# Four small edits at the start of a two-layer hybrid mixer: warm-up matmuls, an activation in front, two small writes elsewhere, modulation units in pairs

## The chip, the cores and the metric

The kernel runs on one core of a Trainium2 chip, as one program. The metric is the device time of one execution in microseconds (us). The median of three runs of the kernel before is 1768.27 us (1764.97 to 1769.26). One more execution was recorded by the profiler.

The engines are TensorE (PE; its weight loads are shown as PEld), VectorE (DVE), ScalarE (ACT), GpSimd (POOL) and SyncE (SP, which only issues DMAs here). DMAs issued by SyncE and by ScalarE appear as SPq and ACTq.

## The reference, cut to what matters

Two layers of a conditioned transformer-like block over 256 context and 256 latent tokens of width 1024. Each layer mixes three branches (a gated delta rule, a gated linear recurrence, a differential attention) and ends in a gated feed-forward. What bears on the change is the conditioning: a vector `c` (and one for the context, `c_ctx`) goes through a SiLU and a matrix of 6 times 1024 columns per layer; the six pieces shift, scale and gate the two sublayers.

```
s_lat = jax.nn.silu(c)
s_ctx = jax.nn.silu(c_ctx)[None]
for l in range(DEPTH):
    mod_l = jnp.split(s_lat @ w_mod[l] + b_mod[l], 6, axis=-1)
    mod_c = jnp.split(s_ctx @ w_mod[l] + b_mod[l], 6, axis=-1)
    u_l = modulate(rmsnorm(h_lat, norm_mix[l]), mod_l[0], mod_l[1])
    u_c = modulate(rmsnorm(h_ctx, norm_mix[l]), mod_c[0], mod_c[1])
    ...
```

Here `modulate(h, shift, scale)` is `h * (1 + scale) + shift`.

## The kernel before, in words

**Layout.** Activations lie feature-major: 8 tiles of 128 features by 512 tokens (256 of the context, then 256 latent). Every product of float32 accuracy is made of three matmuls in a rounded format: high part by high part, high by low, low by high (`gemm`, lines 271 to 273). A weight slab is loaded by SyncE (line 256), its high part is rounded (259) and its low part is the difference (260).

**First stage of layer 0 (lines 446 to 490).** The residual `h` is read in eight loads of 256 KB; ScalarE squares each and VectorE adds the squares up (`Norm.add`). Then come small constants, the conditioning vector (`s_in`, 128 KB), the parameter vectors. `s_act`, the SiLU of the conditioning vector, is made of a tanh on ScalarE (line 460) and two VectorE operations; it needs another table of ScalarE than the square root of the norm. Two DMAs on ScalarE's queue (line 464) write the two columns of `s_act`, 1,024 values of 4 bytes each, to a DRAM tile `sd`. It is read back, broadcast over the partitions, by `mod_steps` (line 328), where VectorE makes the other modulation pieces as row sums: first around 450 us of the span.

The shift and scale of the first sublayer are made by TensorE. Their 2048 columns are eight units of 256. A unit (`mod_unit`) loads 1 MB of weights (`wm`, six buffers), makes 8 matmuls in four column groups of the array (line 306), copies the bank to SBUF (`mev`, one buffer, line 308), makes two transposes (311) and a reduction over the groups (312), and adds the bias. The stage goes by quarters: quarter i takes units i and 4+i, loads the matching quarter of the weights of the first five projections (`w32`, 640 KB, line 475), modulates two of the eight tiles, and then adds that quarter's products to five PSUM banks (`pre`: two of `mm`, two of `pg`, one of `md`). After four quarters the five banks hold five finished projections, and layer 0 goes on with slabs.

**Layer 0 behind that.** The remaining projections of the delta rule, its chunks, then four projections of the recurrence and the rotated q and k of the attention (line 1011 on, `rope`), then the recurrent scans (`lru`), attention, the merge and the feed-forward.

**What sets the order.** The order on each engine is not the order of the text. A scheduler plays the program through with a model of the engines' and transfers' times: an instruction becomes ready when what it needs is done and its tile has a place, and an engine that is free takes the ready instruction that comes first in the text. `high_priority(offset=n)` moves instructions n places ahead for this choice (slab loads 300, modulation matmuls 60); `keep_in_program_order` ties one behind the instruction before it in the text on its engine. On the chip each engine then runs its list strictly in order. DMAs signal their landing on eight counters in turn, and a DMA waits until the one eight places before it has landed.

Of the kernel before, what the change touches and what calls it, by code (L numbers as in the profile page):

```python
# [9 lines left out]
F32 = mybir.dt.float32  # L10
F32R = mybir.dt.float32r
F16 = mybir.dt.float16
AF = mybir.ActivationFunctionType
# [8 lines left out]
YO = (3, 0, 4, 5, 1, 6, 7, 2)  # L22
EARLY = 6
NFIRST = 5
MB = 6
MW = 256
D = 1024
# [146 lines left out]
def build(tc, I, out, dbg=None):  # L174
    nc = tc.nc
    V, S, G, PE, SP = nc.vector, nc.scalar, nc.gpsimd, nc.tensor, nc.sync
# [14 lines left out]
    def nm(s):  # L191
        uid[0] += 1
        return f"{s}_{uid[0]}"

    def tap(name, ap):
        if dbg is not None:
            dbg(name, ap)
# [10 lines left out]
    def bank(tag="dn", dt=F32):  # L208
        return banks["pool"].tile([128, 512], dt, tag=tag, name=nm(tag), bufs=banks["n"][tag])
# [7 lines left out]
    def scope(name, side=None):  # L217
        p = tc.tile_pool(name=nm(name), bufs=1, side=side, reuse_waits="tile")
        q = p.__enter__()
        return q, lambda: p.__exit__(None, None, None)  # L220
# [6 lines left out]
    s_act = cp.tile([128, 8, 32], F32, name="s_act")  # L227
# [8 lines left out]
    def vc(l, name, j=0, n=1):  # L236
        o = l * NVL + _V[name] + j
        return vec[:, o:o + n]
# [46 lines left out]
    def mod_out(l, k0, nb, nv):  # L285

        o = modT[l][:, k0:k0 + nb, 0:nv]
        V.tensor_tensor(o, in0=o, in1=vc(l, "bm", k0, nb).unsqueeze(2).to_broadcast([128, nb, nv]), op=ALU.add)
        c, k = k0 // 8, slice(k0 % 8, k0 % 8 + nb)
        i = c // 3  # L290
        if c % 3 == 1:
            V.scalar_tensor_tensor(amod[l][i][:, k, 0:nv], in0=o, scalar=1.0, op0=ALU.add, op1=ALU.mult,
                                   in1=vc(l, ("nm", "nf")[i], k.start, nb).unsqueeze(2).to_broadcast([128, nb, nv]))
        if c % 3 == 2:
            V.tensor_scalar(gmod[l][i][:, k, 0:nv], in0=o, scalar1=0.5, scalar2=None, op0=ALU.mult)

    def mod_unit(q, tag, p, bufs):

        nb = MW // 128
        wm = p.tile([128, 8, MW], F32, tag="wm", name=nm("wm"), bufs=bufs)  # L300
        SP.dma_start(wm, I["wmod"][:, q * MW:(q + 1) * MW].rearrange("(a p) c -> p a c", p=128))
        ps = bank(tag)[:, :MW]
        with tc.high_priority(offset=60):
            for k in range(8):
                j = 32 * (k % 4)
                PE.matmul(ps[j:j + 32], lhsT=s_act[:, k], rhs=wm[:, k], start=k < 4, stop=k >= 4, tile_position=(0, j))
        ev = p.tile([128, MW], F32, tag="mev", name=nm("mev"), bufs=1)
        S.copy(ev, ps)
        pt = bank(tag)[:, :MW].rearrange("p (b f) -> p b f", f=128)
        for b in range(nb):  # L310
            PE.transpose(pt[:, b], ev[:, b * 128:(b + 1) * 128], ident)
        V.tensor_reduce(modT[0][:, q * nb:(q + 1) * nb], in_=pt.rearrange("p b (g r) -> p b r g", r=32)[:, :, 0:2], op=ALU.add,
                        axis=AX.X)
        mod_out(0, q * nb, nb, 2)

    sd = dp.tile([2, D], F32, name="sd")
# [84 lines left out]
    def new_u():  # L401
        return [[up.tile([128, 512], F32R, tag=t, name=nm(t)) for t in ("uh", "ul")] for _ in range(8)]

    def modulate(u, h, rs, l, which, tk, p, tag="nt", bufs=4, ks=range(8)):

        for k in ks:
            t = p.tile([128, 512], F32, tag=tag, name=nm("nt"), bufs=bufs)
            hi, lo = u[k]
            for sl, i in ((CTX, 1), (LAT, 0)):
                if tk in (ALL, sl):  # L410
                    a = amod[l][which][:, k, i:i + 1]
                    b = modT[l][:, which * 24 + k, i:i + 1]
                    if k % 2 == 0:
                        V.scalar_tensor_tensor(t[:, sl], in0=h[k][:, sl], scalar=a, in1=rs[:, sl], op0=ALU.mult, op1=ALU.mult)
                        S.activation(hi[:, sl], t[:, sl], AF.Identity, bias=b)  # L415
                        V.scalar_tensor_tensor(lo[:, sl], in0=t[:, sl], scalar=b, in1=hi.bitcast(F32)[:, sl], op0=ALU.add,  # L416
                                               op1=ALU.subtract)
                    else:
                        G.tensor_tensor(t[:, sl], in0=h[k][:, sl], in1=rs[:, sl], op=ALU.mult)
                        V.tensor_scalar(t[:, sl], in0=t[:, sl], scalar1=a, scalar2=b, op0=ALU.mult, op1=ALU.add)  # L420
                        S.copy(hi[:, sl], t[:, sl])
                        G.tensor_tensor(lo[:, sl], in0=t[:, sl], in1=hi.bitcast(F32)[:, sl], op=ALU.subtract)
# [18 lines left out]
    def new_h():  # L441
        t = [hp.tile([128, 4, 512], F32, tag="h", name=nm("h")) for _ in range(2)]
        return [t[k // 4][:, k % 4] for k in range(8)]


    sp, done_sp = scope("st")
    s_in = sp.tile([128, 8, 32], F32, name="s_in")
    h = new_h()
    nn = Norm(sp)
    u = new_u()  # L450
    first = ("mm", "mm", "pg", "pg", "md", "dn")[:NFIRST]
    nfst = len(first)
    pre = {n: bank(b) for n, b in enumerate(first)}
    for k in range(8):
        SP.dma_start(h[k], I["hin"][:, k])
        nn.add(k, h[k], ALL)
    SP.dma_start(cst[:, 0:256], I["cst"][:, 0:256])
    SP.dma_start(s_in, I["cc"])
    SP.dma_start(vec, I["vec"])
    S.activation(s_act, s_in, AF.Tanh, scale=0.5)  # L460
    V.scalar_tensor_tensor(s_act, in0=s_act, scalar=1.0, in1=s_in, op0=ALU.add, op1=ALU.mult)
    V.tensor_scalar(s_act, in0=s_act, scalar1=0.5, scalar2=None, op0=ALU.mult)
    for v in range(2):
        S.dma_start(sd[v].rearrange("(k p) -> p k", p=128), s_act[:, :, v])
    V.tensor_copy(id16, ident)
    V.tensor_scalar(neg16, in0=ident, scalar1=-1.0, scalar2=None, op0=ALU.mult)
    for r in HALVES:
# [1 line left out]
    rs, _ = nn.close(ALL)  # L469

    def quarter(i):
        mod_unit(i, "dn", sp, MB)
        mod_unit(4 + i, "dn", sp, MB)
        w32 = sp.tile([128, nfst, 2, 128], F32, tag="w32", name=nm("w32"), bufs=2)
        SP.dma_start(w32, I["w"][0, 0:nfst].rearrange("n p (k c) -> p n k c", k=8)[:, :, 2 * i:2 * i + 2])
        modulate(u, h, rs, 0, 0, ALL, sp, bufs=8, ks=range(2 * i, 2 * i + 2))
        return w32
# [13 lines left out]
    for l in range(L):  # L491
        full = l == 0
# [19 lines left out]
        def proj(n, tk, tag=None):  # L512

            if n in pre:
                return pre.pop(n)
            if tag is None:
                tag = rot[0]
                rot.append(rot.pop(0))
            ps = bank(tag)
            w = tk.stop - tk.start  # L520
            gemm(ps[:, :w], slab(l, n), range(8), u, tk)
            return ps[:, :w]
# [42 lines left out]
        dn, done_dn = scope("dn")  # L565
# [10 lines left out]
        def conv(ps, w, bias, y):  # L576

            n = ps.shape[1] // 256
            xp = xq.tile([128, 2, 260], F32, tag="xp", name=nm("xp"), bufs=2)[:, :n]
            pv = ps.rearrange("p (s t) -> p s t", t=256)  # L580
            yv = y.rearrange("p (s t) -> p s t", t=256)
            G.memset(xp[:, :, 0:1], 0.0)
            G.memset(xp[:, :, 257:259], 0.0)
            S.copy(xp[:, :, 1:257], pv)
            if bias is None:
                S.activation(yv, pv, AF.Copy, scale=w[:, 1:2])  # L586
            else:
                S.activation(yv, pv, AF.Identity, scale=w[:, 1:2], bias=bias)
            for j in (0, 2, 3):
                V.scalar_tensor_tensor(yv, in0=xp[:, :, j:j + 256], scalar=w[:, j:j + 1], in1=yv, op0=ALU.mult, op1=ALU.add)  # L590
# [138 lines left out]
        for j in range(2):  # L729
            p = proj(W_LX + j, ALL)  # L730
# [280 lines left out]
        for j in range(2, 4):  # L1011
            conv(proj(W_LX + j, ALL), vc(l, "lcw", 4 * j, 4), vc(l, "lcb", j), lx[:, j])
            tap(f"lx{l}", lx[:, j])
        for at, t4, tk in ((W_DQ, dq, TK), (W_DK, dk, ALL)):
            for j in range(4):
                rope(proj(at + j, tk), t4[:, j])
                tap(f"dqk{l}", t4[:, j])
# [94 lines left out]
        scale = 64 ** -0.5  # L1112
# [109 lines left out]
        nn = Norm(cq, sq="zs", rs="macc", nsq=1, nrs=2)  # L1222
# [21 lines left out]
        u, pre = by_halves(last, h, nn, l, 1, tks, cq, ((W_FF, "mm"), (W_FF + 1, "dn")), "ya", 8)  # L1244
# [25 lines left out]
        nn = Norm(fp)  # L1270
# [24 lines left out]
        if l == 0:  # L1295
            u, pre = by_halves(last, h, nn, 1, 0, tks, fp, FIRST)
# [34 lines left out]
```

## Time and profile before

| What | Value |
|---|---|
| median of three runs | 1768.27 us |
| profiled execution | 1766.63 us |
| its span, first to last instruction | 1764.8 us |
| granted TensorE clock, mean | 0.979 |
| TensorE matmul busy | 1642.2 us (93%) |
| VectorE busy | 1184.1 us (67%) |
| ScalarE busy | 781.7 us (44%) |
| GpSimd busy | 196.4 us (11%) |
| read from memory | 230.92 MB |

Busy shares are means over the whole span; a change in one stage is read from the rows of that stage. In a row of a timeline stand the start, the time from the first to the last end, engine, line, operation, tiles (out from in), and the number of instructions; in brackets the idle time of the engine ahead of it and what ended it. In a chain of waits stand start, length and what the time was spent on.

### The profile page before, as it was taken

The numbers are of one execution on the slowest core, as the hardware profiler recorded it, in microseconds if no ns is written. First come the engines' busy times: TensorE is split into PE (matmuls) and PEld (weight loads), VectorE is DVE, ScalarE is ACT, GpSimd is POOL, SyncE is SP. The second block draws the span as 40 slices with busy tenths as digits, with TensorE's granted clock in tenths as the row PEclk, the third lists the DMA queues.
The fourth block names the chain that finished last, engine by engine and source line by source line (L and its number), as shares of the span: only waits on it lengthen the run. The fifth ranks groups of instructions, "written<-read, shape, count | busy, mean of one in ns | idle before, by whom it ended". The sixth has DMA issues, their size and how long they took to land.

```text
span 1764.8 us, 28759 instructions
## 1 busy us (share of the span) xinstructions
PE 1642.2 (93%) x11346; PEld 1365.6 (77%) x11346; DVE 1184.1 (67%) x2033; ACT 781.7 (44%) x1326; POOL 196.4 (11%) x266
## 2 busy tenths in 40 slices
PE   4898999899999998999999999989999999989997
PEld 2676787567777887777778888767787599989997
DVE  4578665586887746899883337776666775765554
ACT  4475653656422234322223224667545634444443
POOL 1211100000310004111111003011000002111100
PEclk8999999999999998999999999999999999989999
DMA  9433101221655434566872334332113145545554
GB/s 243 142 132 98 44 20 41 96 71 37 196 180 179 161 113 137 179 200 206 278 235 93 107 107 145 108 128 66 50 38 111 48 142 187 185 146 187 183 180 131
DMA packets 100343, 235.18 MB, mean 133 GB/s; under 512 B 11072, under 2 KB 36556, under 8 KB 99568
## 3 DMA queue, kind: packets, MB, share of 16 engines
q1 hardware_dynamic: 88928, 228.46, 40.3%
q10 hardware_dynamic: 11280, 4.89, 1.2%
q8 instruction: 89, 1.46, 0.3%
q14 instruction: 46, 0.38, 0.1%
HBM read 230.92 MB, written 2.39 MB: 132 GB/s over the span
## 4 chain that ended last, share of the span: by engine, by line
PE 47%; DVE 18%; issue 16%; DMA 10%; ACT 5%; POOL 2%; SPq 1%; POOLq 0%; DVEq 0%; ACTq 0%
PE mm L272 7%; PE mm L273 7%; PE mm L271 7%; DVE md L347 5%; PE dn L273 4%; PE dn L271 4%; PE dn L272 4%; DVE wl L260 4%; DMA mwm<-in_wmt 3%; PE dn L802 2%; PE dn L816 2%; DMA f<-in_wmt 2%; PE pp L1061 1%; DMA wm<-in_wmod 1%; PE dn L913 1%
## 5 line engine op out<-in xcount | busy, mean ns | idle before, releaser
L260 DVE TENSOR_TENSOR wl<-wr,wh 128x1024 fp32r<-128x1024 f32 (+1 forms) x299 | 368.3, 1232 | 228.4 <-PE dn L273 91.6
L259 ACT CAST wh<-wr 128x1024 fp32r<-128x1024 f32 (+1 forms) x241 | 249.2, 1034 | 360.1 <-PE dn L272 184.9
L273 PE MATMUL mm<-uh,wl 128*128 128x512 f32 (+1 forms) x1048 | 372.1, 355 | 17.2 <-DVE wl L260 17.0
L271 PE MATMUL mm<-uh,wh 128*128 128x512 f32 (+1 forms) x1048 | 372.6, 355 | 4.3 <-ACT uh L415 2.5
L272 PE MATMUL mm<-ul,wh 128*128 128x512 f32 (+1 forms) x1048 | 370.3, 353 | 2.5 <-DVE ul L416 2.1
L273 PEld LDWEIGHTS mm<-uh,wl 128*128 128x128 f32 x1048 | 201.2, 192 | 48.8 <-DVE wl L260 24.1
L271 PEld LDWEIGHTS mm<-uh,wh 128*128 128x128 f32 x1048 | 201.6, 192 | 32.4 <-issue 6.4
L272 PEld LDWEIGHTS mm<-ul,wh 128*128 128x128 f32 x1048 | 201.4, 192 | 32.4 <-issue 6.7
L273 PE MATMUL dn<-uh,wl 128*128 128x512 f32 (+1 forms) x448 | 153.2, 342 | 1.5 <-DVE wl L260 1.5
L271 PE MATMUL dn<-uh,wh 128*128 128x512 f32 (+1 forms) x448 | 152.7, 341 | 0.0
L272 PE MATMUL dn<-ul,wh 128*128 128x512 f32 (+1 forms) x448 | 152.6, 341 | 0.0
L347 DVE SCALAR_TENSOR_TENSOR md<-mwm,sb 128x512 f32<-128x512 f32 x160 | 124.4, 778 | 14.5 <-DMA mwm<-in_wmt 10.9
L273 PEld LDWEIGHTS dn<-uh,wl 128*128 128x128 f32 x448 | 86.0, 192 | 13.4 <-DVE wl L260 4.5
L272 PEld LDWEIGHTS dn<-ul,wh 128*128 128x128 f32 x448 | 86.1, 192 | 9.2
L271 PEld LDWEIGHTS dn<-uh,wh 128*128 128x128 f32 x448 | 86.2, 192 | 8.7
L347 DVE SCALAR_TENSOR_TENSOR md<-f 128x512 f32<-128x512 f32 x96 | 76.1, 792 | 19.2 <-DMA f<-in_wmt 14.0
L277 POOL TENSOR_TENSOR hid<-ft,hid 128x512 fp32r<-128x512 f32 (+1 forms) x44 | 50.9, 1158 | 332.9 <-ACT hid L276 332.9
L276 ACT CAST hid<-ft 128x512 fp32r<-128x512 f32 (+1 forms) x44 | 22.6, 514 | 121.2 <-DVE ft L1267 121.2
L259 DVE CAST wh<-wr 128x1024 fp32r<-128x1024 f32 x61 | 43.2, 710 | 46.2 <-PE mm L272 39.5
L271 PE MATMUL pg<-uh,wh 128*128 128x512 f32 (+1 forms) x176 | 65.6, 373 | 3.5 <-ACT ta L586 3.5
L273 PE MATMUL pg<-uh,wl 128*128 128x512 f32 (+1 forms) x176 | 65.0, 369 | 2.0 <-DVE wl L260 2.0
L272 PE MATMUL pg<-ul,wh 128*128 128x512 f32 (+1 forms) x176 | 64.8, 368 | 0.0
(383 smaller groups left out, 3320.6 us busy)
## 6 DMA issues: line engine op xcount, KB each, us to landing
wr<-in_w SPq DMA_DIRECT2D x284, 512.0 KB, 3.5
mwm<-in_wmt SPq DMA_DIRECT2D x112, 256.0 KB, 3.9
f<-in_wmt SPq DMA_DIRECT2D x48, 256.0 KB, 2.7
wm<-in_wmod SPq DMA_DIRECT2D x8, 1024.0 KB, 9.8
wr<-in_w SPq DMA_DIRECT2D x18, 384.0 KB, 3.2
r<-rd SPq DMA_DIRECT2D x5, 1024.0 KB
ta<-gd ACTq DMA_DIRECT2D x12, 256.0 KB, 3.6
w<-in_w SPq DMA_DIRECT2D x4, 640.0 KB, 11.1
```

Of the source, the lines that this page charges most:

```text
L259: (eh.copy if eh is S else eh.tensor_copy)(hi[:, k], r32[:, k])
L260: el.tensor_tensor(lo[:, k], in0=r32[:, k], in1=hi.bitcast(F32)[:, k], op=ALU.subtract)
L271: PE.matmul(ps, lhsT=hi[:, k], rhs=xh[:, tk], start=first and i == 0, stop=False)
L272: PE.matmul(ps, lhsT=hi[:, k], rhs=xl[:, tk], start=False, stop=False)
L273: PE.matmul(ps, lhsT=lo[:, k], rhs=xh[:, tk], start=False, stop=last and i == n - 1)
L276: S.copy(hi, y)
L277: (eng or G).tensor_tensor(lo, in0=y, in1=hi.bitcast(F32), op=ALU.subtract)
L347: V.scalar_tensor_tensor(junk, in0=wm[i % len(wm)], scalar=1.0, in1=sb[:, 0 if nh == 1 else h, v], op0=ALU.mult, op1=ALU.mult, accum_out=o)
L802: PE.matmul(p[:, j], lhsT=lhs[:, j], rhs=rhs[:, j], start=True, stop=True)
L816: PE.matmul(p[r, d, j], lhsT=lhs[r, d, j], rhs=rhs[r, d, j], start=True, stop=True, tile_position=(64 * n, 64 * n))
L913: PE.matmul(p[:, j], lhsT=cb[:, d, j], rhs=x0[d][:, j], start=True, stop=False)
L1061: PE.matmul(p[:, n], lhsT=gw[:, n, j], rhs=lx[:, j], start=True, stop=True)
```

## The change

It has four parts, all but one of them in the first stage.

1. Warm-up: a tile `wz` of 128 by 512 16-bit zeros is set by VectorE, and 40 matmuls of it by itself are written into the first bank of `pre` before anything else on TensorE. The first projection's own first matmul starts that bank afresh.
2. The load of `s_in` is the first load of all, and the tanh is tied to its place in the text, ahead of the norm's table load and squares. The norm object, and with it the preload of the square root's table, comes behind it.
3. The two writes of `s_act` to `sd` leave the first stage; they are written in layer 0, between the last projections of the recurrence and those of the attention's q and k. They stay on ScalarE's queue and have no order forced on them.
4. `mod_unit` is cut into `mod_rows` (load, matmuls, copy; two buffers of `mev`) and `mod_turn` (transposes, reduction, bias). A quarter calls `mod_rows` for both of its units, then `mod_turn` for both.

```diff
+WARM = 40
...
-    def mod_unit(q, tag, p, bufs):
+    def mod_rows(q, tag, p, bufs):
...
-        ev = p.tile([128, MW], F32, tag="mev", name=nm("mev"), bufs=1)
+        ev = p.tile([128, MW], F32, tag="mev", name=nm("mev"), bufs=2)
         S.copy(ev, ps)
+        return ev
+
+    def mod_turn(q, ev, tag):
+        nb = MW // 128
         pt = bank(tag)[:, :MW].rearrange("p (b f) -> p b f", f=128)
...
-    nn = Norm(sp)
...
+    wz = sp.tile([128, 512], F16, name="wz")
+    V.memset(wz, 0.0)
+    for i in range(WARM):
+        PE.matmul(pre[0], lhsT=wz[:, 0:128], rhs=wz, start=True, stop=True)
+    SP.dma_start(s_in, I["cc"])
+    tc.keep_in_program_order(S.activation(s_act, s_in, AF.Tanh, scale=0.5))
+    nn = Norm(sp)
     for k in range(8):
         SP.dma_start(h[k], I["hin"][:, k])
         nn.add(k, h[k], ALL)
     SP.dma_start(cst[:, 0:256], I["cst"][:, 0:256])
-    SP.dma_start(s_in, I["cc"])
     SP.dma_start(vec, I["vec"])
-    S.activation(s_act, s_in, AF.Tanh, scale=0.5)
     V.scalar_tensor_tensor(s_act, in0=s_act, scalar=1.0, in1=s_in, op0=ALU.add, op1=ALU.mult)
     V.tensor_scalar(s_act, in0=s_act, scalar1=0.5, scalar2=None, op0=ALU.mult)
-    for v in range(2):
-        S.dma_start(sd[v].rearrange("(k p) -> p k", p=128), s_act[:, :, v])
...
     def quarter(i):
-        mod_unit(i, "dn", sp, MB)
-        mod_unit(4 + i, "dn", sp, MB)
+        rows = [mod_rows(q, "dn", sp, MB) for q in (i, 4 + i)]
+        for q, ev in zip((i, 4 + i), rows):
+            mod_turn(q, ev, "dn")
...
             conv(proj(W_LX + j, ALL), vc(l, "lcw", 4 * j, 4), vc(l, "lcb", j), lx[:, j])
             tap(f"lx{l}", lx[:, j])
+        if full:
+            for v in range(2):
+                S.dma_start(sd[v].rearrange("(k p) -> p k", p=128), s_act[:, :, v])
         for at, t4, tk in ((W_DQ, dq, TK), (W_DK, dk, ALL)):
```

## Rows read from the trace of the kernel before

**Rows 1.** The page: span, and TensorE's busy time, share and instructions.

```profile
span 1764.8 us, 28759 instructions
...
PE 1642.2 (93%) x11346; PEld 1365.6 (77%) x11346; DVE 1184.1 (67%) x2033; ACT 781.7 (44%) x1326; POOL 196.4 (11%) x266
```

**Rows 2.** Busy times by stretch: PE, PEld, DVE, ACT, POOL, PEclk, DMA share, GB/s.

```profile
0.00:18.50 18.50, 5.54 (x26) 2.88 (x26) 7.74 (x25) 11.73 (x17) 1.11 (x6) 1.00 0.92 301
18.50:36.70 18.20, 8.43 (x47) 4.71 (x47) 5.97 (x18) 4.15 (x12) 3.40 (x5) 0.72 1.06 137
36.70:61.00 24.30, 20.28 (x126) 13.61 (x130) 12.27 (x32) 10.09 (x24) 8.54 (x8) 1.00 1.02 345
61.00:77.00 16.00, 14.22 (x84) 9.59 (x77) 8.32 (x22) 6.23 (x15) 1.70 (x6) 1.00 0.01 2
```

**Rows 3.** Chain of waits of the stretch 0 to 82 us: start, length, what.

```profile
13.21 23.45 DMA wm<-in_wmod
...
36.80 1.07 PE dn L306 x16
...
76.88 0.24 PE md L273
```

**Rows 4.** DMA queues from 18.5 to 36.7 us: packets, MB, share of 16 engines.

```profile
q1 hardware_dynamic: 2133, 2.49, 88.6%
q10 hardware_dynamic: 1787, 0.01, 17.4%
```

**Rows 5.** Timeline of ScalarE from 0 to 80 us, five rows.

```profile
12.27 1.28 ACT L384 ACT_TABLE_LOAD   x1
13.41 0.39 ACTq L464 DMA_DIRECT2D sd<-s_act  x1
13.56 0.26 ACT L384 ACTIVATE r<-dn,vec 128x4 f32<-128x4 f32 x1
13.84 0.59 ACTq L464 DMA_DIRECT2D sd<-s_act  x1
...
15.76 0.29 ACT L629 ACTIVATE sm<-vec 128x1 f32<-128x1 f32 x2
```

**Rows 6.** Timeline of TensorE from 10 to 36 us, four rows.

```profile
11.50 1.87 PE L382 MATMUL dn<-cst,nacc 128*128 128x1 f32 x8 [11.50 <-DVE nacc L374]
...
28.99 1.93 PE L306 MATMUL dn<-wm,s_act 128*32 128x256 f32 x16 [4.97 <-DMA wm<-in_wmod]
...
33.16 0.63 PE L273 MATMUL mm<-uh,wlo 128*128 128x512 f32 x1
...
33.58 0.63 PE L271 MATMUL mm<-uh,whi 128*128 128x512 f32 x1
```

**Rows 7.** Early issues, by source line: lambda vectors, old residual, its first reader.

```profile
L1091 ACTq DMA_DIRECT2D da<-in_dal x2: 357/372/387, 308.6 to 1328.7; - x2
...
L1218 DVE SCALAR_TENSOR_TENSOR h<-mm,gm,old x12: 474/478/483, 647.1 to 1552.6; 128x256 f32<-128x256 f32 x12
...
L1227 SPq DMA_DIRECT2D old<-in_hin x11: 327/382/512, 450.5 to 691.6; - x11
```

**Rows 8.** Timeline of SyncE's queue from 0 to 80 us, two rows.

```profile
28.59 8.66 SPq L301 DMA_DIRECT2D wm<-in_wmod  x2
...
54.55 0.42 SPq L489 DMA_DIRECT2D cst<-in_cst  x1
```

**Rows 9.** Timeline of TensorE from 59 to 72 us, three rows.

```profile
60.67 1.07 PE L306 MATMUL dn<-wm,s_act 128*32 128x256 f32 x16
...
64.18 1.07 PE L306 MATMUL dn<-wm,s_act 128*32 128x256 f32 x16
...
69.12 0.74 PE L271 MATMUL mm<-uh,whi 128*128 128x512 f32 x2 [1.58 <-ACT uh L415]
```

**Rows 10.** Waits of SyncE's queue, 0 to 80 us: us in total, times, longest.

```profile
SPq L301 <- DMA sd<-s_act: 7.5, 2, 6.4
```

**Rows 11.** Chain of waits of the stretch 300 to 330 us: start, length, what.

```profile
307.38 6.11 DMA gw<-in_gw
```

More of the change, by code (lines that the diff above doesn't have):

```diff
@@ L295, in mod_out @@
             V.tensor_scalar(gmod[l][i][:, k, 0:nv], in0=o, scalar1=0.5, scalar2=None, op0=ALU.mult)
-    def mod_unit(q, tag, p, bufs):
-        nb = MW // 128
+    def mod_rows(q, tag, p, bufs):
         wm = p.tile([128, 8, MW], F32, tag="wm", name=nm("wm"), bufs=bufs)
```

## The prediction

> **What bounds the kernel now.** I read first the page's busy line, then the busy times by stretch of the first 77 us, then the chain of waits there, and last the queues and single engines inside the one stretch that stood out. The page says that TensorE is busy 93% of the span [rows 1], so over the whole kernel the time is matmul time, and only a stretch in which TensorE waits can give anything back. All four edits sit in the first stage (layer 0's first modulation and its first five projections, up to about 77 us), so the stretches of that stage are what matters [rows 2]. The reader is to see three things there. From 0 to 18.5 us the DMA engines move 301 GB/s and TensorE has little to do. From 18.5 to 36.7 us they are just as busy (share above 1) but move only 137 GB/s, and TensorE works 8.43 of 18.2 us. From 36.7 to 61 us they are back at 345 GB/s, and after 61 us they are idle while TensorE works 14.22 of 16 us.
>
> The chain of waits names the joint between the two halves [rows 3]: one 1 MB load of modulation weights is under way from 13.21 us for 23.45 us; when it lands, the modulation matmuls of unit 5 start at 36.80 us, and from there to the last matmul of the stage, which ends at 77.1 us, no DMA is on the chain any more. So the stage is: landing of the fourth modulation load (36.7 us) plus 40.3 us of matmuls, conversions and short bubbles.
>
> Why that load is so slow: in the stretch 18.5 to 36.7 us a second queue is open with 1,787 packets that together hold 0.01 MB [rows 4]. These are the two writes of the conditioning vector to DRAM (two times 1,024 values of 4 bytes), which ScalarE issues at 13.41 and 13.84 us [rows 5]. The big queue moved 2.49 MB meanwhile; at the 345 GB/s of the next stretch that takes 7.2 us instead of 18.2. The small writes thus cost about 11.0 us of DMA time, and these lie on the chain.
>
> **The change part by part.** Sums are made against the profiled execution (1766.63 us; its span is 1764.8 us, with 1.83 us around it); the median of the runs shown, 1768.27 us, is 1.64 us above it.
>
> *The small writes moved in the text to layer 0's q and k projections.* If they really went out there, the 11.0 us would be free. But the kernel's order is made by a scheduler that takes what is ready when an engine has nothing better, and the trace shows how far it reaches: an exponential of layer 0 and the same one of layer 1 (line 629) both run at 15.76 us [rows 5], the second one long before its layer, which is the last of the span; the load of the attention's lambda vectors, written behind both recurrent scans, is issued from ScalarE's queue at 308.59 us, ahead of them; the loads of the old residual are issued from 450.5 us and read first at 647.1 us [rows 7]. The two writes need nothing but the finished conditioning vector, and they hold no tile that could make them wait. The vector is now finished early. So I expect them to be issued about as soon as it is, between the squares of the norm, 13.41 us at the latest, and to do the same harm a few us earlier. Against this stands one row: a load of constants that needed nothing at all (line 489) left SyncE's queue only at 54.55 us, behind all the loads of the stage [rows 8]; but that queue was never without a load that came earlier in the text, and ScalarE's is. Bytes and small packets that lie ahead of the fourth modulation load are the same in either order, so its landing at 36.7 us stays: 0 us, between -11.0 (the writes are away) and +6.4 (the slow rival below). I take 0.
>
> *Conditioning activation in front.* ScalarE loses the table load for the tanh and the one back to the square root (1.28 us from 12.27 us; the square root runs at 13.56 us [rows 5]) and gains one ahead of the squares, at a time when it waits for the first load anyway. The norm's eight matmuls end at 11.50 + 1.87 = 13.37 us [rows 6], so the square root can come 0.2 us earlier. The unit that follows waits for loads, so this is worth 0, at most -0.2.
>
> *Warm-up.* 40 matmuls of 512 columns into a bank that the projections overwrite later. TensorE is idle until 11.50 us [rows 6]. Matmuls of 512 columns follow each other at 0.42 us at the lower of the two clock levels (33.16 to 33.58 us [rows 6]) and at 0.24 us at the higher (the chain's last row [rows 3]), so 40 take 9.6 to 16.8 us; from about 1 us on they end between 11 and 18 us, at worst some 6 us into the norm's chain. That chain has this room: the modulation matmuls of unit 1 wait 4.97 us for their load until 28.99 us [rows 6], and unit 5's until 36.80. What the warm-up could give is the difference in the matmuls that ran at half clock: unit 1's matmuls took 1.93 us where unit 5's took 1.07 [rows 3, 6], and some ten projections lost 0.19 us each: 2.8 us. They lie in front of the wait for unit 5's load, which swallows them. I take 0, between -2.8 and +1. The zeroing of the tile is one VectorE operation beside the first loads: nothing.
>
> The granted clock shows what would become of the warmth: its mean is 0.72 from 18.5 to 36.7 us [rows 2], after TensorE had been waiting for loads. The Trainium skill ("TensorE: Matmul & The Clock Gate", section "Why this matters for your kernels") says in other words that a clock once raised is lost again when the engine idles between bursts; by this rule the warm-up is worth 0 at 28.99 us, and if the warmth held it would be -2.8 us at most. The trace agrees with the rule: the drop comes in the stretch with the waits.
>
> *First units paired.* Both units' matmuls and copies are now written ahead of both transposes, with two buffers for the copy. For the first two quarters the loads set the pace. In the last quarter unit 3's matmuls start at 60.67 us and unit 7's at 64.18 us although all loads are in, and TensorE then idles 1.58 us before the quarter's first projection at 69.12 us [rows 9]. If unit 7 follows at once (at 61.74), everything behind it may come 2.4 us earlier, and bubbles of 1.58 us here and at most 1.5 us in the third quarter (not shown by a row of its own; an estimate by the same wait) can close. The matmuls between them must still run. I take -2.0 us, between -3.1 and 0 (the scheduler already orders by readiness, and may give the same order as now).
>
> *The load of the conditioning vector first on SyncE's queue.* 128 KB ahead of the 2 MB of the residual: 0.4 us later first square, hidden by the same slack. 0.
>
> Sum: 0 + 0 + 0 - 2.0 + 0 and -0.5 for the rest of the small edges (half of the room between 0 and -1): -2.5 us. 1766.63 - 2.5 = 1764.1 us for the profiled execution, 1765.8 us by the median. The kernel's measurement can tell changes from about 0.3%, 5.3 us, so this is no change.
>
> **The rivals.**
>
> *The writes do leave the front.* For it: the text puts them behind the whole recurrent block of layer 0, and the row of line 489 [rows 8] shows that a late place in the text can hold a transfer back while loads are queued. Against it: the three early issues of rows 5 and 7. Then the fourth modulation load lands at 36.7 - 11.0 = 25.7 us and the 40.3 us follow from there. At the new place they would lie beside a load of 512 KB for the recurrent gates that is on the chain with 6.11 us [rows 11]; at 137 GB/s it takes 3.8 us of moving where 345 GB/s take 1.5, so up to 2.3 us come back. -11.0 - 2.5 + 2.3 = -11.2; without the collision -13.5. By the median 1755 to 1757 us, and I take 1757. The Trainium skill ("DMA: Bandwidth & Descriptors", section "Issuing engines are not separate DMA queues") says that transfers started by different engines share the same DMA engines and interleave; by this rule the new place helps only by its time, and ScalarE's own queue shields nothing. The trace agrees: 137 GB/s beside the second queue.
>
> *The writes hold back a load that the chain needs.* SyncE's loads already wait for the landing of these writes: 7.5 us in two waits, the longer 6.4 us [rows 10]; today it is the third pair of modulation loads (28.59 us [rows 8]), which nothing needs before 48 us. Issued some five to eight us earlier, the writes are waited for by an earlier load of the queue. If that is the fourth modulation load or the second quarter's projection weights, the joint of the chain moves by up to that wait: 36.7 + 6.4 = 43.1 us, and the sum is +6.4 - 2.5 = +3.9, by the median 1772 us. It decides once the load held back lands after 36.7 us. Against it: the writes would also be over earlier.
>
> *The pairing changes nothing, and the warm-up holds up the norm.* The scheduler gives the same order, and the 40 matmuls run at the lower level to 18 us. The first quarter then starts later, but unit 5's load still sets the joint: 0 to +1, 1768 to 1769 us. This is within the forecast's own range.
>
> **How the numbers follow.** The forecast (writes still in the front, small gain) has 0.66, with an own range of 1760 to 1770 us; writes away 0.22; a load held back 0.12. The range reaches down to 1755, which takes in most of the second case, and up to 1771, which takes in about half of the third. Faster by over 0.3% (below 1763 us): a fifth of the forecast's own spread (0.13) and nearly all of the second case (0.21), 0.34. Slower (above 1773.6 us): 0.03 of the forecast and two thirds of the third case, 0.11. Within: 0.55.
>
> **What would show it.** Right: two DMA issues of the conditioning vector on ScalarE's queue before 14 us, a stretch of about 17 us with well under 200 GB/s at a full DMA share before 37 us, unit 5's matmuls still near 36 us, and unit 7's close behind unit 3's. Wrong: 340 GB/s without a break until about 50 us and the projections' first slab matmul (line 271 on a tile of the normal slabs) near 65 us instead of 77; then the writes were moved in fact. If unit 5's matmuls start after 40 us and SyncE waits for the conditioning vector ahead of a modulation load, the slow rival holds. If the granted clock is full from 18 to 37 us and the stage ends earlier by more than 3 us with the slow stretch still there, I have undervalued the warm-up.

## The result and the profile after

The changed kernel takes 1784.01 us (median of 7 runs, 1777.09 to 1792.04) where the kernel before takes 1768.27 us (7 runs beside it, 1764.97 to 1775.15): a ratio of 1.0083, 95% interval 1.0066 to 1.01. It is 0.8% slower, some 15 us. The forecast was no change (1765.8 us, range 1755 to 1771). The profiled execution of the changed kernel took 1777.09 us, the fastest of its runs, so its trace shows less of the loss than the median.

The page of the changed kernel answers to [rows 1]: TensorE is busy for 11 us more, about what the warm-up takes (10.32 us, in a row below), and its share stays at 93%.

```profile
span 1775.3 us, 28844 instructions
...
PE 1653.3 (93%) x11386; PEld 1369.6 (77%) x11386; DVE 1185.7 (67%) x2034; ACT 783.3 (44%) x1327; POOL 197.8 (11%) x266
```

Busy times by stretch, the columns of [rows 2]:

```profile
0.00:18.50 18.50, 10.32 (x40) 4.22 (x40) 6.55 (x23) 10.50 (x15) 0.20 (x4) 0.89 0.89 194
18.50:36.70 18.20, 10.98 (x62) 5.09 (x62) 4.72 (x18) 4.11 (x12) 1.41 (x2) 0.55 0.95 253
36.70:61.00 24.30, 20.39 (x119) 13.23 (x119) 12.83 (x36) 11.23 (x28) 8.78 (x10) 1.00 1.01 340
61.00:77.00 16.00, 13.17 (x71) 8.50 (x71) 6.95 (x19) 3.90 (x11) 3.94 (x5) 0.89 0.00 2
```

The slow stretch of the loads has moved forward: 194 GB/s where there were 301 up to 18.5 us, and 253 instead of 137 behind it. The warm-up fills TensorE in the first stretch, and the granted clock of the second is lower than before (0.55 against 0.72).

The chain of waits of 0 to 82 us, and its continuation (start, length, what; [rows 3]):

```profile
9.14 20.42 DMA wm<-in_wmod
29.69 3.64 PE dn L306 x28
...
82.39 0.23 PE md L274
```

The stage's last matmul starts at 82.39 us, 5.5 us later than the 76.88 of before. The chain's load is no longer unit 5's but one of the first quarter, landing at 29.6 us.

DMA queues of the changed kernel from 0 to 18.5 us (packets, MB, share; [rows 4] has the stretch behind):

```profile
q1 hardware_dynamic: 2622, 3.58, 82.5%
q10 hardware_dynamic: 1698, 0.01, 6.6%
```

The 4-byte packets of the conditioning vector now lie among the norm's loads. ScalarE's timeline, 0 to 25 us ([rows 5]; the bracket is the idle time before a row and what ended it):

```profile
5.92 0.42 ACTq L1023 DMA_DIRECT2D sd<-s_act  x1
...
8.45 0.37 ACTq L1023 DMA_DIRECT2D sd<-s_act  x1
...
10.59 1.28 ACT L636 ACT_TABLE_LOAD   x1
16.64 0.20 ACT L636 ACTIVATE sm<-vec 128x1 f32<-128x1 f32 x1 [4.77 <-DMA vec<-in_vec]
16.75 0.62 ACT L377 ACTIVATE nsq<-h 128x512 f32<-128x512 f32 x1
...
20.81 0.27 ACT L388 ACTIVATE r<-dn,vec 128x4 f32<-128x4 f32 x1 [2.06 <-PE dn L386]
```

Both writes leave early, as forecast, between the squares (L377). But the exponentials of alog (L636, line 629 before) now stand ahead of the last square and of the norm's square root (L388), where they wait for a load. VectorE, 4 to 20 us:

```profile
8.30 1.49 DVE L378 TENSOR_TENSOR nacc<-nacc,nsq 128x512 f32<-128x512 f32 x2 [0.93 <-ACT nsq L377]
15.67 0.23 DVE L471 CAST id<-cst 128x128 f16<-128x128 f32 x1 [5.88 <-DMA cst<-in_cst]
```

The cast of the identity stands ahead of the norm's last additions and waits 5.88 us for the constants, which come behind the small packets. TensorE, 0 to 40 us ([rows 6]):

```profile
1.19 10.32 PE L460 MATMUL mm<-wz 128*128 128x512 f16 x40 [1.19 <-DVE wz L458]
18.91 1.87 PE L386 MATMUL dn<-cst,nacc 128*128 128x1 f32 x8 [7.40 <-DVE sm L637]
...
29.69 3.64 PE L306 MATMUL dn<-wm,s_act 128*32 128x256 f32 x28 [4.55 <-DMA wm<-in_wmod]
...
37.03 0.73 PE L272 MATMUL mm<-uh,whi 128*128 128x512 f32 x2 [1.19 <-ACT uh L419]
...
40.04 1.07 PE L306 MATMUL dn<-wm,s_act 128*32 128x256 f32 x16
```

The warm-up ends at 11.5 us, the norm's matmuls start at 18.91 us (before: 11.50) and the first projection at 37.03 us (before: 30.85, on a row not shown). Unit 5's matmuls start at 40.04 us (before: 36.80) and no longer wait for their load. This is one delay; what it costs is measured below (e8). A second lies far behind the edited code, in layer 0's convolutions of the delta rule. VectorE, 130 to 146 us, in the changed kernel:

```profile
134.21 0.68 DVE L622 SCALAR_TENSOR_TENSOR sv<-tb,ta 128x512 f32<-128x512 f32 x1
140.99 0.75 DVE L597 SCALAR_TENSOR_TENSOR ta<-xp,vec,ta 128x512 f32<-128x512 f32 x1 [6.10 <-ACT ta L593]
```

ScalarE, 128 to 148 us, says why: between the row at 133.11 us and the awaited `ta<-pg` come two table loads and seven operations of the decays (L719).

```profile
134.63 1.28 ACT L542 ACT_TABLE_LOAD   x1
...
136.63 1.28 ACT L719 ACT_TABLE_LOAD   x1
137.92 0.41 ACT L719 ACTIVATE f<-f,bcol 128x128 f32<-128x128 f32 x1
...
140.21 0.68 ACT L593 ACTIVATE ta<-pg,vec 128x512 f32<-128x512 f32 x1
```

In the kernel before, no wait of VectorE in 105 to 160 us is as long as 2 us.

### The profile page after: what moved, and what is told of

Same layout as the page of the kernel before. It is cut to its first block, busy times and chain, and to the rows that moved or that the text cites. A ratio compares the mean times of both kernels' runs of the same rounds, so it can differ in the third digit from the quotient of the medians.

```text
span 1775.3 us, 28844 instructions
## 1 busy us (share of the span) xinstructions
PE 1653.3 (93%) x11386; PEld 1369.6 (77%) x11386; DVE 1185.7 (67%) x2034; ACT 783.3 (44%) x1327; POOL 197.8 (11%) x266
## 4 chain that ended last, share of the span: by engine, by line
PE 48%; issue 17%; DVE 17%; DMA 9%; ACT 5%; POOL 2%; SPq 0%; ACTq 0%; POOLq 0%; DVEq 0%
PE mm L273 7%; PE mm L274 7%; PE mm L272 7%; PE dn L274 4%; PE dn L272 4%; PE dn L273 4%; DVE md L351 4%; DVE wl L261 4%; DMA mwm<-in_wmt 2%; PE dn L809 2%; DMA f<-in_wmt 2%; PE dn L823 2%; PE pp L1071 1%; DMA wm<-in_wmod 1%; PE dn L920 1%
```

## The experiments

All times are medians of several runs, each with runs of the kernel before on the same chip; "stage" is the start of the last matmul on `md` before 100 us, against the kernel before's 76.72; "clock" is the mean granted clock of the timed runs (before: 0.981 to 0.982; the last section says what this mean leaves out).

| kernel | us | ratio, 95% interval | stage, us | clock |
|---|---|---|---|---|
| after | 1784.01 | 1.0083 [1.0066, 1.01] | +5.5 | 0.974 |
| e1_after_pinned | 1774.25 | 1.0046 [1.003, 1.0062] | -3.3 | 0.977 |
| e2_before_pinned | 1758.72 | 0.996 [0.9937, 0.9982] | -8.7 | 0.983 |
| e3_before_front | 1775.87 | 1.0048 [1.0033, 1.0063] | +4.8 | 0.981 |
| e4_before_warm | 1780.78 | 1.0075 [1.0058, 1.0091] | +2.6 | 0.975 |
| e5_warm_oldorder | 1770.81 | 1.0028 [1.0015, 1.004] | +2.3 | 0.978 |
| e6_after_pinned_oldorder | 1764.46 | 0.9991 [0.9978, 1.0003] | -2.8 | 0.980 |
| e7_after_oldorder | 1771.96 | 1.0036 [1.0023, 1.0049] | +6.5 | 0.977 |
| e8_front_oldorder | 1767.67 | 1.0009 [0.9998, 1.0021] | +6.8 | 0.984 |
| e9_warm8 | 1765.77 | 1.0 [0.999, 1.001] | +2.3 | 0.979 |
| e10_warm32 | 1768.46 | 1.0013 [1.0, 1.0025] | +2.3 | 0.979 |
| e11_pair_alone | 1768.88 | 1.0012 [1.0, 1.0023] | +3.1 | 0.980 |
| e12 (pinned, no warm-up) | 1765.87 | 0.9998 [0.9986, 1.0009] | -2.8 | 0.982 |
| e13_writes_wide | 1754.94 | 0.9941 [0.9923, 0.996] | -6.6 | 0.984 |
| e14 (front, writes tied early) | 1767.56 | 1.0013 [0.9998, 1.0028] | +2.3 | 0.982 |
| e15_move_in_text | 1764.06 | 1.0002 [0.9986, 1.0019] | +0.4 | 0.981 |
| e16_pinned_thirdorder | 1764.42 | 1.0 [0.9984, 1.0016] | -7.8 | 0.981 |
| e17_writes_as_rows | 1761.5 | 0.9979 [0.9966, 0.9993] | -3.6 | 0.983 |
| e18_front_layer0_writes | 1765.14 | 1.0 [0.9984, 1.0016] | -2.6 | 0.983 |

The stage's end and the time do not go together one to one: e8's stage is 6.8 us late and its time 0.09% longer, e18's is 2.6 us early and its time is that of before.

**The parts alone.** Theory A: the writes, issued among the norm's loads, make the loss. B: warm-up or pairing. C: the scheduler's order further behind. e1 and e2 tie the writes to their new place in the text (in the changed kernel and in the kernel before); e3 and e4 add to the kernel before only the conditioning in front, or only the warm-up.

```diff
-                S.dma_start(sd[v].rearrange("(k p) -> p k", p=128), s_act[:, :, v])
+                tc.keep_in_program_order(S.dma_start(sd[v].rearrange("(k p) -> p k", p=128), s_act[:, :, v]))
```

```diff
+    SP.dma_start(s_in, I["cc"])
+    tc.keep_in_program_order(S.activation(s_act, s_in, AF.Tanh, scale=0.5))
     nn = Norm(sp)
...
-    SP.dma_start(s_in, I["cc"])
...
-    S.activation(s_act, s_in, AF.Tanh, scale=0.5)
```

```diff
+    wz = sp.tile([128, 512], F16, name="wz")
+    V.memset(wz, 0.0)
+    for i in range(WARM):
+        PE.matmul(pre[0], lhsT=wz[:, 0:128], rhs=wz, start=True, stop=True)
```

> The changed kernel, with the two small writes tied behind the instruction ahead of them in the text on ScalarE, so that they really leave in layer 0 at about 300 us. Theory A (the loss is the writes, which left at 5.9 and 8.5 us, inside the norm's loads, and kept the 4-byte packets on the way of everything behind): without them there the first stage ends near 65 us instead of 82, and the time is 1755 to 1760 us, below the kernel before. Rival B (the 40 warm-up matmuls or the pairing cost the time): the loss of about 15 us stays, 1775 to 1785 us, less at most the 11 us of small writes: not below 1770. Rival C (the order further behind changed for the worse): 1768 to 1775 us.

> The kernel before, with only the two small writes taken from the first stage and tied to the place in layer 0 that the change names. This measures the small writes alone: 1757 us if the 11.0 us of slow loads lie on the chain as I worked out (1768 minus 11, with up to 2.3 us back beside the gate weights), 1768 us if the first stage is bound by something else.

> The kernel before, with only the conditioning vector loaded first and its tanh in front; the small writes stay where they stand in the text and become ready early. Theory A: they leave between the squares at about 6 and 9 us, as in the changed kernel, so the time is as bad, 1776 to 1785 us. Rivals B and C: no loss, 1766 to 1770 us.

> The kernel before with only the zeroed tile and the 40 warm-up matmuls. Theory A: no loss, 1766 to 1770 us, since the matmuls end near 11.5 us, when the norm's first matmul can start. Rival B: 1775 us or more. Rival C (any edit shifts the scheduler's order further behind): 1770 to 1775 us.

e2 did what the change was written for: with the writes issued at 162 us its loads run without a break, here the stretch 18.5 to 36.7 us by the columns of [rows 2].

```profile
18.50:36.70 18.20, 14.88 (x100) 8.64 (x92) 11.74 (x34) 9.46 (x24) 5.71 (x7) 1.00 1.09 358
```

The stage ends 8.65 us early and the kernel is 0.4% faster. But e1, with its stage 3.3 us early, is still slower than before, and the warm-up alone (e4) costs 13 us with a stage only 2.6 us late. A alone falls. In e1, e3, e4 and the changed kernel VectorE has the same 6.1 us hole in the convolutions (6.08, 6.09, 6.08 and 6.10 us), and in all four the exponentials of alog stand ahead of the norm's square root.

**The order.** e5 to e8 are e4, e1, the changed kernel and e3, each with one edit: the exponential may be placed only behind the norm's square root. It adds no wait; behind the first stage ScalarE's and VectorE's instructions then stand in the order of before, but for a few rows of ScalarE. Without the tie, the orders of the changed kernel and of before differ on these engines between about 77 and 290 us.

```diff
+            roots.append(S.activation(r, ps[:, :n], AF.Sqrt, scale=1.0 / D, bias=cc("eps6")))
...
+        after_root(S.activation(nal, vc(l, "alog"), AF.Exp))
```

> The kernel before with the 40 warm-up matmuls, and with layer 0's exponential of alog tied behind the norm's first square root, so that the scheduler's order behind the first stage is the one of the kernel before. Theory C (the warm-up costs by the order that it makes the scheduler choose in layer 0, 110 to 150 us, about 9 to 12 us): 1766 to 1769 us, within 0.3% of before. Theory B (the warm-up itself costs, through what it does to the clock): 1777 to 1782 us, as e4_before_warm.

> e1_after_pinned with the same tie: conditioning in front, warm-up and paired units, the writes tied to layer 0 at about 300 us, order behind the first stage as before. Theory C with A (writes are worth 8 us, the new order costs 9 to 12): 1755 to 1762 us. Theory B (warm-up and front edits cost by themselves): about 1774 us, as e1_after_pinned.

> The changed kernel with the same tie and nothing else: the writes still leave among the norm's loads, the order behind the first stage is as before. If two causes add (the writes in front of the norm's loads cost 5 us at the end of the first stage, the order the rest): 1771 to 1776 us. If the order is all: 1766 to 1769. If the order is nothing: 1782 to 1786, as the changed kernel.

> The kernel before with the conditioning's load and activation in front (and so the writes free to leave early), with the same tie. e3_before_front was 4.8 us late at the end of the first stage and 7 at 150 us. If what the writes do to the norm's loads makes this: 1771 to 1774 us, 3 to 5 us over before. If the order makes it: 1766 to 1769.

In every pair the old order is faster: by 0.47 points of the ratio (e4 to e5), 0.55 (e1 to e6), 0.47 (after to e7) and 0.39 (e3 to e8), on average 0.47% or 8.3 us. VectorE's hole is gone in all four. ScalarE of e7, 129 to 146 us, has the awaited `ta<-pg` ahead of the table loads:

```profile
134.79 0.68 ACT L599 ACTIVATE ta<-pg,vec 128x512 f32<-128x512 f32 x1
135.48 1.28 ACT L548 ACT_TABLE_LOAD   x1
```

Where the loss arises can be read from a row that every version has, the square of the delta rule's result on ScalarE. Here it is in the profiled executions of before, the changed kernel, e7, e4 and e5, in this order:

```profile
308.58 1.91 ACT L527 ACTIVATE sq<-oacc 128x2048 f32<-128x2048 f32 x1 [2.60 <-DVE f L1008]
```

```profile
318.31 1.91 ACT L534 ACTIVATE sq<-oacc 128x2048 f32<-128x2048 f32 x1 [2.60 <-DVE f L1015]
```

```profile
313.32 1.91 ACT L540 ACTIVATE sq<-oacc 128x2048 f32<-128x2048 f32 x1 [2.60 <-DVE f L1021]
```

```profile
318.54 1.91 ACT L532 ACTIVATE sq<-oacc 128x2048 f32<-128x2048 f32 x1 [2.60 <-DVE f L1013]
```

```profile
309.48 1.91 ACT L538 ACTIVATE sq<-oacc 128x2048 f32<-128x2048 f32 x1 [2.60 <-DVE f L1019]
```

Against its partner with the old order the changed kernel is 5.0 us behind at this row and e4 9.1 us, though their stages ended 1.0 us before and 0.3 us behind the partners'. So the new order costs 6.0 and 8.8 us between the stage's end and 310 us (e1 to e6: 11.4, e3 to e8: 4.5). These are single executions; their mean, 7.7 us, is most of the 8.3 us.

From 130 to 170 us the changed kernel, then e7 (columns of [rows 2]):

```profile
130.00:170.00 40.00, 28.04 (x140) 21.25 (x139) 30.79 (x46) 26.04 (x57) 7.88 (x22) 0.83 0.27 90
```

```profile
130.00:170.00 40.00, 31.96 (x219) 23.99 (x219) 35.26 (x54) 27.88 (x58) 6.86 (x22) 0.91 0.33 109
```

TensorE is busy for 31.96 us there in e7 and for 28.04 us in the changed kernel, and at a higher granted clock (0.91 against 0.83). So C holds for more than half of the loss, but not for all: e7 is still 0.36% (6.4 us) slower than before, and its stage ends 6.5 us late. e7 came as expected for two causes that add, and e8 as expected if the order is all. e5 and e6 came some 2 us above what theory C expected.

**Dose of the warm-up, and pairing alone.** e9 and e10 are e4 with `WARM = 8` and `WARM = 32`, where the old order stays by itself; e11 has only the pairing; e12 is e6 with `WARM = 0`.

```diff
-        mod_unit(i, "dn", sp, MB)
-        mod_unit(4 + i, "dn", sp, MB)
+        rows = [mod_rows(q, "dn", sp, MB) for q in (i, 4 + i)]
+        for q, ev in zip((i, 4 + i), rows):
+            mod_turn(q, ev, "dn")
```

> The kernel before with 8 warm-up matmuls in place of 40 (the order behind the first stage stays that of before). With 40 of them and that order the mean granted clock fell from 0.982 to 0.978 and the time rose by 5 us. If the 512-column matmuls are paid for by the clock later in the kernel, a fifth of them costs about 1 us: 1765 to 1769 us, clock about 0.981. If any warm-up at all sets off the loss: about 1771, clock 0.978.

> The kernel before with 32 warm-up matmuls: one less than where the scheduler's order flips would be enough to keep before's order with no tie. If the order is what costs most with 40 (1780.8 us) and the clock the rest: 1768 to 1772 us, clock about 0.978. If the warm-up costs by itself, without the order: 1777 to 1781.

> The kernel before with only the first modulation units paired (order behind the first stage as before). The prediction took 2 us off the end of the first stage for it: 1763 to 1766 us. If the loads end the stage whatever the units do: 1765 to 1768.

> e6_after_pinned_oldorder without the warm-up matmuls: conditioning in front, paired units, the writes tied to layer 0, order as before. If the parts add (writes -7, conditioning and pairing about 0, no warm-up): 1757 to 1760 us, clock 0.981 to 0.983. If the warm-up was worth something to the first stage: 1763 to 1767, no better than e6.

In the old order 8, 32 and 40 warm-up matmuls cost 0.00, 0.13 and 0.28%. All three end the stage 2.3 us late, so the difference among them arises later. Between 32 and 40 it is within the intervals, and the mean clock does not tell the three apart (0.979, 0.979 and 0.978). The row of `sq<-oacc` in e5 is 0.9 us behind that of before, so the 5 us of e5 do not show in the first 310 us; their cause stays open. Pairing gave no gain, and the paired units did not move together: TensorE, 46 to 76 us, in e11:

```profile
63.85 1.07 PE L305 MATMUL dn<-wm,s_act 128*32 128x256 f32 x16
67.39 1.07 PE L305 MATMUL dn<-wm,s_act 128*32 128x256 f32 x16
72.26 0.73 PE L271 MATMUL mm<-uh,whi 128*128 128x512 f32 x2 [1.58 <-ACT uh L418]
```

Unit 7 follows unit 3 by 3.54 us ([rows 9]: 3.51), and the bubble of 1.58 us is still there. Unit 1's matmuls start at 29.50 us ([rows 6]: 28.99) behind the same loads, and the stage ends 3.1 us late; the time is above both expectations for e11. e12 missed: 1757 to 1760 us was expected and 1765.87 came, with or without the warm-up the same (e6). Something in front other than the writes held this family back.

**The writes themselves, and the conditioning in front.** e13 leaves the writes where they were and makes their pieces 32 bytes (the values go out in another order, so it does not compute the reference); e14 was meant as e8 with the writes in layer 0, but the edit tied them behind the squares, at 11.47 us; e15 only moves their text; e16 is e2 with a third order.

```diff
-        S.dma_start(sd[v].rearrange("(k p) -> p k", p=128), s_act[:, :, v])
+        S.dma_start(sd.rearrange("v (q x) -> (v q) x", x=16)[:, 8 * v:8 * v + 8], s_act.rearrange("p a v -> p (a v)")[:, 8 * v:8 * v + 8])
```

```diff
-        S.activation(nal, vc(l, "alog"), AF.Exp)
+        tc.keep_in_program_order(S.activation(nal, vc(l, "alog"), AF.Exp))
```

> The kernel before with its two writes at their place, of the same 8 KB, but in 32-byte pieces (256 of them) in place of 2,048 of 4 bytes; the vector is written in another order, so the modulations read from it later are not the reference's. If the number of pieces is what takes the loads' time: end of the first stage 6 to 9 us earlier, loads near 345 GB/s in the stretch 18.5 to 36.7, time 1757 to 1761 us, as e2_before_pinned. If the place of the writes in the queue or their wait is what costs: as before, 1765 to 1768.

> Conditioning in front and the writes tied to layer 0, order as before; no warm-up and no pairing. e12 with pairing ended the first stage 2.8 us early, e2 8.65 us early. If pairing's 3.1 us (e11) make half of the difference: first stage 5.5 to 6 us early, 1759 to 1763 us. If the conditioning in front makes all of it: 2.8 us early, about 1765.

> The kernel before with only the writes' text moved to layer 0, nothing tied. By the prediction the scheduler still issues them as soon as the vector is there, so nothing changes: first stage within 1 us of before, 1764 to 1768 us. If the text place holds them: 1757 to 1761, as e2_before_pinned.

> e2_before_pinned with layer 0's exponential of alog fixed at its place in the text, which gives a third order of the instructions behind the first stage (neither the one of before nor the one of the changed kernel). If before's order is merely better than the changed one: somewhere between 1758.7 (e2) and 1767. If orders scatter: 1753 to 1767; a time under 1757 would be a better version than both kernels and e2.

e13, window 18.5 to 36.7 us:

```profile
18.50:36.70 18.20, 16.64 (x96) 9.49 (x92) 11.76 (x32) 9.45 (x24) 4.95 (x6) 1.00 1.08 359
```

The same 8 KB at the same place, in 288 packets instead of 2,080 on that queue (0 to 40 us): full rate, and 0.59% faster. So the jam comes from the cutting into pieces (their number and their size changed together) and not from the bytes or the place. e15 agrees with the forecast: moving the text moves nothing (issues at 13.95 and 14.38 us). e14 says nothing on layer 0; with the writes just behind the squares it has their jam (133 GB/s) and the time of before. e16 kept a stage 7.8 us early and lost all of it again: its order too has a hole in the convolutions, though no run shows that this hole is the loss. VectorE of e16, 105 to 160 us:

```profile
126.98 3.60 DVE L588 SCALAR_TENSOR_TENSOR ta<-xp,vec,ta 128x512 f32<-128x512 f32 x5 [4.58 <-ACT ta L584]
```

e17 computes all and writes the vector as 16 rows of 512 bytes, from the old place; e18 is what e14 was meant to be (writes issued in layer 0).

```diff
+    sr, sw = sp.tile([128, 16], F32, name="sr"), sp.tile([16, 128], F32, name="sw")
+    V.tensor_copy(sr.rearrange("p (v k) -> p k v", v=2), s_act[:, :, 0:2])
+    pt = bank("dn")[:16, 0:128]
+    PE.transpose(pt, sr, ident)
+    V.tensor_copy(sw, pt)
+    S.dma_start(sd.rearrange("v (k p) -> (v k) p", p=128), sw)
```

> The kernel before with its vector turned by one transposition on TensorE and written in 16 pieces of 512 bytes at the old place, in the right order for its readers; alog's exponential tied behind the norm's square root (order behind the first stage as before). If the pieces are the cost (e13: 256 pieces, 1754.9 us): first stage 6 to 9 us early, 1753 to 1759 us, a full version faster than both kernels. If e13 gained only by writing other values or another place: 1763 to 1768.

> Conditioning in front and the writes really tied to layer 0 (about 165 us), order as before; no warm-up, no pairing. Set against e2 (same without the conditioning in front, first stage 8.65 us early, 1758.7 us) and e12 (with pairing too, 2.8 us early, 1765.9). If pairing's 3.1 us make the larger part: first stage 5.5 to 7 us early, 1759 to 1762. If the conditioning in front does: 3 to 4 us early, 1763 to 1766.

e17 has the full rate (359 GB/s) and is 0.21% faster than before, but its turn of the vector stands ahead of the norm's matmuls, which start at 13.85 us, and the stage gains only 3.6 us. Its expectation (1753 to 1759) was missed; e2 has the lowest ratio of the versions that compute all, though its interval and that of e17 overlap. e18 settles e12: the conditioning in front takes the gain by itself. VectorE of e18, 0 to 17 us:

```profile
11.04 0.23 DVE L469 CAST id<-cst 128x128 f16<-128x128 f32 x1 [0.89 <-DMA cst<-in_cst]
11.18 0.68 DVE L380 TENSOR_TENSOR nacc<-nacc,nsq 128x512 f32<-128x512 f32 x1
...
12.99 0.69 DVE L380 TENSOR_TENSOR nacc<-nacc,nsq 128x512 f32<-128x512 f32 x1
```

and TensorE of e18, 0 to 33 us:

```profile
13.74 1.87 PE L388 MATMUL dn<-cst,nacc 128*128 128x1 f32 x8 [13.74 <-DVE nacc L380]
```

With the two operations on the conditioning vector done at 4 us, the scheduler fills VectorE with the casts of the constants, ahead of three of the norm's additions. The constants land at 11.0 us, so the norm starts at 13.74 us (e2: 11.82 us). In the changed kernel the same cast waits until 15.67 us, as the small packets hold up the constants too.

## Why the prediction was wrong

The step that failed is the first one: "All four edits sit in the first stage", so only that stage was priced. The largest part of the loss, 0.47% or 8.3 us, lies behind it, in an order of layer 0 that stood in no term. Of the priced terms the warm-up's bound and the pairing's gain failed too. By term:

- *Writes moved in the text.* The mechanism held: they were issued as soon as the vector was there, at 5.92 and 8.45 us, and the jam of about 18 us came with them. What failed is "do the same harm a few us earlier": the forecast watched the fourth modulation load alone. At the earlier place the packets lie beside the loads of the residual, the constants, the small vectors and the first quarter's modulation weights. The norm's matmuls start 7.4 us later, and the load that the chain waits for is one of the first quarter, which lands at 29.6 us; behind it more of the stage is still to do than behind the fourth. With the writes beside the squares and no order effect (e8) the stage ends 6.8 us late; with them just behind (e14) 2.3 us. For the time, the "0 us" was nearly right: e8 is 0.09% [-0.02, 0.21] slower.
- *Conditioning in front: "worth 0, at most -0.2".* I counted ScalarE's table loads and forgot what the scheduler would do with VectorE's freed place. It costs 1.9 us at the norm's start, 6.1 us at the stage's end and 0.4% of the time once the writes are away (e2 to e18).
- *Warm-up: "I take 0".* Its length was right (10.32 us), and its gain was rightly put at nothing: the norm's matmuls that follow it wait 7.40 us, and the granted clock is 0.55 from 18.5 to 36.7 us. The bound of +1 on the other side was too small: 0.28% [0.15, 0.40], about 5 us, in the old order, and 13 us with the order that it sets off.
- *Pairing: "-2.0 us".* "If unit 7 follows at once" did not come true: it follows by 3.54 us, and the bubble of 1.58 us stayed, as the forecast's own remark on the scheduler allowed. The stage ended 3.1 us later, and the time rose by 0.12% [0.0, 0.23].
- *What was in no term.* The forecast took every edit to act where it is written. The largest term, 8.3 us on average, is an order of layer 0 between about 77 and 290 us that no edit names: two small exponentials that fall ahead of the norm's square root, and then ScalarE's list in the convolutions puts two table loads and the decays before the evacuation that VectorE waits for.
- *The rivals.* The slow one (a load held back that the chain needs) had the right sign with a chance of 0.12, but by another way. Its sign came half: unit 5's matmuls start after 40 us (40.04), but SyncE's queue nowhere waits for the conditioning vector. The late load is one of the first quarter, slowed beside the packets and not held back in the queue. That the slow side came true is therefore luck for this rival. "The writes really leave the front", priced at 1757, is what e2 measured (1758.72), once the writes were tied; the change doesn't tie them.

The sum for the loss of 0.83% is then 0.47% for the order and 0.36% [0.23, 0.49] for the rest (e7), which the parts measured alone cover: conditioning in front with early writes 0.09% [-0.02, 0.21], warm-up 0.28% [0.15, 0.40], pairing 0.12% [0.0, 0.23]. They aren't independent: with the writes away, the conditioning costs 7 us (e2 to e18) and the other two nothing more (e12, e6).

Open: how the 8.3 us divide between the hole in the convolutions, other rows of the new order up to 310 us, and a lower clock there; no run moved that one row of ScalarE alone. Open too is what the warm-up costs by itself in e5, and why pairing ends the stage later. Why the exponentials' place changes an order 60 us later lies in the scheduler, and only the tie was tried.

## What to carry to other kernels

Where a scheduler places the instructions, moving a line may move nothing unless it is tied (e15), and a harmless edit in front can change the order of a stage behind it: compare the order of each engine far beyond the edit before judging the edit, and look for new waits of an engine on another (here 6.1 us of VectorE on ScalarE). Write a vector to DRAM in long pieces, or at a time when no load is waited for. A stage that ends late is not yet a kernel that takes longer (e8): measure both.

## What was not expected of the hardware

2,048 pieces of 4 bytes (8 KB) next to big loads cut these from about 350 to 137 GB/s for 18 us [rows 2]; the same bytes in 256 pieces cost nothing that the trace shows (359 GB/s). The Trainium skill ("DMA: Bandwidth & Descriptors", section "Rules for kernel authors") says to rearrange a transfer so that its last dimension is contiguous, since a strided one becomes one descriptor per element; e13 and e17 agree (2,080 packets became 288 in e13), and they show that the price is paid by the transfers beside it.

The mean granted clock of a run needs care. The busy times of e8 by stretch give a clock of 1.00 from 18.5 to 36.7 us (the columns of [rows 2]):

```profile
18.50:36.70 18.20, 9.10 (x44) 3.06 (x48) 5.75 (x20) 6.12 (x16) 2.21 (x3) 1.00 0.95 267
```

But the units of modulation matmuls that start in that stretch take 1.94 and 1.93 us, and the first that takes 1.07 us starts at 41.45 us:

```profile
28.82 1.94 PE L306 MATMUL dn<-wm,s_act 128*32 128x256 f32 x16 [3.19 <-DMA wm<-in_wmod]
...
36.27 1.93 PE L306 MATMUL dn<-wm,s_act 128*32 128x256 f32 x16
...
41.45 1.07 PE L306 MATMUL dn<-wm,s_act 128*32 128x256 f32 x16
```

These are the lower and the higher level. The trace's records of the clock begin with its first rise, at 40.4 us in e8, 18.1 in the kernel before and 4.3 in the changed kernel, and the time ahead of them is counted as full. So the 0.984 of e8 is no sign of a faster TensorE, and a warm-up lowers the mean in part only because the records begin earlier. That early matmul work is paid for by clock later is not shown: in the profiled executions the mean from 77 us to the end is 0.98 with 8, 32 and 40 warm-up matmuls (e9, e10, e5) as in the kernel before.
